# Partial sums by plain loads, earlier stream loads and spaced side work in a parallel retention and pooling layer

## The chip, the core and the metric

The kernel runs on one core of one Trainium2 chip. The metric is device time in microseconds (us) of the whole program. One execution was also taken by the hardware profiler, and all rows of the trace come from it.

## What is computed

The input is x, 2048 rows of 1024 numbers, in float32. With h the RMS norm of x, a projection gives six groups of 1024 columns: q, k, v, g_ret, u and g_pool.

```python
h = rms_norm(x, pre_g)
q, k, v, g_ret, u, g_pool = split(h @ w_in, 6)
y_ret = retention_branch(q, k, v, positions, ret_norm_g) * silu(g_ret)
y_pool = pooling_branch(u, pool_w, pool_scale) * silu(g_pool)
y = concatenate([y_ret, y_pool]) @ w_out
return x + rms_norm(y, post_g)
```

Retention has 8 heads of 128 columns: a rotary turn of q and k by the positions, products within chunks of 128 rows, a state carried from chunk to chunk, and a norm for each head. Pooling takes, for each quarter of u, a causal mean over 2, 4, 8 or 16 rows less the value itself, and multiplies it with a 256x256 matrix pool_w.

## The kernel before

**Units.** The sequence is cut into four blocks of 512 rows. The large products are done in units. A unit makes a 2x2 arrangement of 128x512 results with seven products in place of eight (a Strassen form), so it needs sums of its operands: S1, S2, S3 and S4. A product is 4 contraction tiles, and each is three matmuls of 128x512, since a float32 operand is split into an upper and a lower part (`split`, L142: ScalarE copies the upper part, VectorE subtracts it). So a unit is 7 x 4 x 3 = 84 matmuls of 512 columns.

**Phases.** There are four phases, and `line` lists their units in order. Phase 0 does blocks 0 and 1 (24 units: 16 for heads, 8 for pooling), phase 1 does blocks 2 and 3 (24 units). Phase 2 multiplies the first half of y with `w_out` for all rows (8 units) and stores partial sums in the DRAM tensor `part`. Phase 3 does the second half (8 units), adds `part`, and finishes the rows: the sum of squares, the norm, x added, the store to `out`. The first two units of phase 0 are done by `first()` (L829) in an order written out by hand (`manual_schedule`). All the rest is ordered by a planner: it takes the order of the program as priority, and puts an instruction into its engine's queue when by its own costs the operands and buffers are there. On the chip each queue is in order and waits where an operand is late.

**The loop** (L1080). For a unit it runs seven places, `at` = 0 to 6, with the products 6, 2, 5, 7, (1 of the next unit), 4, 3. After each product, `slot()` runs what was put off to this place by `later(i, f)` (i places on), then the chore listed for this place, and then `nxt.prep(at)`, the sums and splits of the next unit. At `at` = 6 it calls `load()` for the unit after the next: plain loads by the queue of SyncE (SP), and two accumulating DMAs by GpSimd (POOL), which add a second quadrant onto S1 and S3. `prep(0)` then adds S2 = S1 + "11" on VectorE.

**Buffers.** Operands of units (raw quadrants, sums, lower parts) live in 13 tiles `X`. Nearly everything else lives in 16 tiles `T`: rotated q and k, copies from PSUM, folds, results. A load waits in SP's queue until its tile is free.

**Chores of phase 0** prepare later phases, each in one go at its place in `chores` (L1067). `fold_pool_weights(g)` multiplies pool_w into the projection of u (four times; loads, splits with the lower part on POOL, 48 matmuls of 256 columns, copies by ScalarE, stores). `stats_next(b)` loads the rows of block 2 or 3 and squares them on ScalarE. `tables(b)` makes cosines and sines: eight VectorE steps, three on ScalarE. `combine_h(j)` scales transposed tiles of x for phase 1 and stores seven combinations into `made`; `combine_o` (in phase 1) does the like for `w_out`, for phases 2 and 3. When the phase changes, `after.fetch` loads and splits the seven resident operands of the new phase.

**Phase 3.** For the first seven units, `total(q)` copies or subtracts a result out of PSUM into a tile `ot`, and lets POOL accumulate `part` onto it by a DMA (L686). Two places later come the squares (L681) and `finish`: the norm (L715 to L726), x added by an accumulating DMA of POOL (L732), and right behind it the store `out` on SP's queue (L733). The last unit has a variant: `fetch` loads `part` plainly, `adjust` (L677, POOL) subtracts it from the two saved terms u2 and x5, and the other two results take it in a VectorE addition (`total_last`, L700).

**The saved terms.** Product 6's bank is corrected in place (L322) and copied to u2 by ScalarE (L324), then product 7 accumulates into the same bank. Product 5's bank is copied to x5 (L331), then product 3 accumulates into it.

Of the kernel before, what the change touches and what calls it, by code (L numbers as in the profile page):

```python
# [9 lines left out]
F32 = mybir.dt.float32  # L10
# [71 lines left out]
def layer_kernel(ctx: ExitStack, tc: tile.TileContext, x, xt, pos, wt, wut, wo, pw, cols, postg, const, out):  # L82
# [126 lines left out]
    def combine_tile(n, j, b11, b12, b21, b22, keep):  # L209

        s = slice((j % 2) * BLK, (j % 2 + 1) * BLK)

        def put(p, t):
            nc.gpsimd.dma_start(out=made[n, p][j // 2][:, s], in_=t)

        def op(p, a, b, alu):
            t = T(f"c{n}{p}{j}")[:, :BLK]
            nc.vector.tensor_tensor(out=t, in0=a, in1=b, op=alu)
            put(p, t)
            return t  # L220
        if keep:
            for p, t in ((1, b11), (2, b21), (3, b22)):
                put(p, t)
        t1 = op(5, b11, b12, ALU.subtract)
        t2 = op(6, b22, t1, ALU.add)
        op(7, b12, b22, ALU.subtract)
        op(4, b21, t2, ALU.subtract)

    def combine_h(j, b0, b1):
# [4 lines left out]
        for name, b, k in (("b11", b0, j), ("b12", b1, j), ("b22", b1, KH + j), ("b21", b0, KH + j)):  # L234
            nc.vector.scalar_tensor_tensor(out=t[name], in0=t[name], scalar=col[:, k:k + 1], in1=rb[b],
                                           op0=ALU.mult, op1=ALU.mult)
        combine_tile(1, j, t["b11"], t["b12"], t["b21"], t["b22"], True)

    def combine_o(n, j):
# [5 lines left out]
        combine_tile(n, j, t["b11"], t["b12"], t["b21"], t["b22"], False)  # L245


    class Unit:
        def __init__(self, name, quads, uses):
            self.name, self.quads, self.uses = name, quads, uses  # L250
            self.op, self.bank = {}, {}
            self.fetch = self.adjust = None

        def load(self):
            self.raw = {}

            def land(name, q):
                t, view = X(f"{name}_{self.name}"), self.quads[q]
                dst = t if len(view.shape) == 2 else t.rearrange("p (f t) -> p f t", f=KH)
                nc.sync.dma_start(out=dst, in_=view)  # L260
                self.raw[name] = t
                return dst
            s1 = land("S1", "21")
            s3 = land("S3", "11")
            nc.gpsimd.dma_start(out=s1, in_=self.quads["22"], accum_op=ALU.add)
            nc.gpsimd.dma_start(out=s3, in_=self.quads["21"], accum_op=ALU.add)
            for q in ("11", "12", "22"):
                land(q, q)
# [11 lines left out]
        def prep(self, i):  # L280
            raw = self.raw
            if i == 0:
# [856 lines left out]
```

## Time and profile before

| | us |
|---|---|
| median of 3 runs | 1624.98 (1624.18 to 1631.08) |
| time of the profiled execution | 1622.46 |
| its span, from first to last instruction | 1620.6 |
| TensorE (PE) busy in the span | 1473.8 |
| VectorE (DVE) busy | 1044.2 |
| ScalarE (ACT) busy | 722.6 |
| GpSimd (POOL) busy | 500.0 |

The mean granted clock of TensorE is 0.967 of 2.4 GHz. Two things are read from such a profile: where TensorE idles and what it waited for, stage by stage, and where its clock fell to the lower level behind such a wait.

### The profile page before, as it was taken

The page shows a single profiled execution, that of the slowest core. Times are in us where ns is not written, and L with a number is a line of the kernel's source. Part 1 is how long each engine was busy: PE and PEld are TensorE (multiplying, and loading weights), DVE is VectorE, ACT ScalarE, POOL GpSimd, SP SyncE. Part 2 cuts the span into 40 slices and gives each one's busy share as a digit, 9 for nine tenths or more (in the row PEclk, how much of TensorE's full clock was granted, in tenths as well). Part 3 has the DMA queues.
Part 4 walks back from the last instruction along what each step waited for, and adds up shares of the span by engine and source line. Part 5 has one row for each costly group of instructions (what it writes and reads, how often), then busy time and mean ns, then how long its engine had stood idle before and what let it go on. Part 6 is the DMA issues. An engine that isn't in the chain of part 4 may idle for free. (4 is left out here: it accounts for less than half of the span.)

```text
span 1620.6 us, 20953 instructions
## 1 busy us (share of the span) xinstructions
PE 1473.8 (91%) x6976; PEld 1209.9 (75%) x6976; DVE 1044.2 (64%) x2166; ACT 722.6 (45%) x1383; POOL 500.0 (31%) x529
## 2 busy tenths in 40 slices
PE   4998979898989999799999999999996999987875
PEld 3777767687878888588888887887885888766664
DVE  6983736775757766876777667677677544645354
ACT  5554535445344434454444444344444433533331
POOL 0223231325252425522223314233245221133333
PEclk9999999999999999799999999999998999998987
DMA  8134544546454546544455535554456655887976
GB/s 309 41 78 124 150 111 109 151 131 173 140 155 133 162 123 173 180 116 105 117 156 149 161 82 148 144 162 108 121 153 191 177 155 144 286 194 149 221 163 175
DMA packets 115372, 243.80 MB, mean 150 GB/s; under 512 B 14016, under 2 KB 14144, under 8 KB 115264
## 3 DMA queue, kind: packets, MB, share of 16 engines
q1 hardware_dynamic: 75264, 149.12, 28.3%
q0 software_dynamic: 40000, 93.35, 26.4%
q8 instruction: 55, 0.90, 0.2%
q14 instruction: 53, 0.43, 0.1%
HBM read 187.88 MB, written 54.53 MB: 150 GB/s over the span
## 5 line engine op out<-in xcount | busy, mean ns | idle before, releaser
L312 PE MATMUL b_o<-rh,h_o 128*128 128x512 f32 x192 | 82.9, 432 | 40.3 <-ACT u_o L324 24.6
L431 POOL TENSOR_TENSOR sw_q<-sw_q,sin 128x512 f32<-128x512 f32 x32 | 50.6, 1583 | 144.7 <-ACT sw_q L429 98.8
L312 PE MATMUL b_up<-rh,h_up 128*128 128x512 f32 x192 | 78.7, 410 | 18.0 <-DVE gp L336 13.4
L443 POOL DMA_DIRECT2D yd<-sg x32 | 25.0, 780 | 196.3 <-DVE r L487 145.1
L312 PE MATMUL b_qk<-rh,h_qk 128*128 128x512 f32 x180 | 74.3, 413 | 10.7 <-DVE rot_k L336 5.6
L313 PE MATMUL b_o<-rl,h_o 128*128 128x512 f32 x192 | 81.2, 423 | 0.5 <-DVE rl L145 0.5
L314 PE MATMUL b_o<-rh,l_o 128*128 128x512 f32 x192 | 80.7, 420 | 0.0
L517 ACT ACTIVATE on<-op,sh,y_o 128x128 f32<-128x128 f32 x128 | 48.1, 456 | 72.7 <-DVE sh L514 72.7
L312 PEld LDWEIGHTS b_o<-rh,h_o 128*128 128x128 f32 x192 | 39.4, 205 | 54.8 <-ACT u_o L324 27.5
L313 PE MATMUL b_up<-rl,h_up 128*128 128x512 f32 x192 | 77.5, 404 | 0.0
L314 PE MATMUL b_up<-rh,l_up 128*128 128x512 f32 x192 | 77.4, 403 | 0.0
L313 PE MATMUL b_qk<-rl,h_qk 128*128 128x512 f32 x180 | 72.6, 403 | 0.0
L312 PE MATMUL b_vg<-rh,h_vg 128*128 128x512 f32 x180 | 72.3, 402 | 0.2 <-DVE rot_q L430 0.2
L314 PE MATMUL b_qk<-rh,l_qk 128*128 128x512 f32 x180 | 72.3, 402 | 0.0
L314 PE MATMUL b_vg<-rh,l_vg 128*128 128x512 f32 x180 | 70.5, 392 | 0.0
L313 PE MATMUL b_vg<-rl,h_vg 128*128 128x512 f32 x180 | 70.3, 391 | 0.0
L624 POOL TENSOR_TENSOR w<-ub 128x527 f32<-128x527 f32 x32 | 41.3, 1290 | 86.8 <-issue 41.1
L624 POOL TENSOR_TENSOR w<-w 128x525 f32<-128x525 f32 (+2 forms) x48 | 66.5, 1386 | 2.4
L145 DVE TENSOR_TENSOR rl<-m,rh 128x1024 fp32r<-128x1024 f32 x42 | 57.3, 1369 | 15.3 <-ACT rh L144 13.5
L431 POOL TENSOR_TENSOR sw_k<-sw_k,sin 128x512 f32<-128x512 f32 x32 | 49.8, 1557 | 56.1 <-ACT sw_k L429 53.0
L312 PEld LDWEIGHTS b_up<-rh,h_up 128*128 128x128 f32 x192 | 37.7, 197 | 28.8 <-DVE gp L336 15.3
L661 POOL DMA_DIRECT2D part<-pt_o x32 | 17.6, 552 | 108.9 <-ACT pt_o L349 65.7
(507 smaller groups left out, 4820.1 us busy)
## 6 DMA issues: line engine op xcount, KB each, us to landing
m<-made SPq DMA_DIRECT2D x30, 512.0 KB, 6.0
made<-c POOLq DMA_DIRECT2D x48, 256.0 KB, 4.0
yd<-sg POOLq DMA_DIRECT2D x32, 256.0 KB, 2.8
S_up<-in_wt POOLq DMA_DIRECT2D x32, 256.0 KB, 5.6
yd<-mx POOLq DMA_DIRECT2D x32, 256.0 KB, 2.8
b<-in_wo SPq DMA_DIRECT2D x32, 256.0 KB, 4.0
S_o<-yd SPq DMA_DIRECT2D x32, 256.0 KB, 4.0
S_o<-yd POOLq DMA_DIRECT2D x32, 256.0 KB, 5.9
```

The source lines that it names most:

```text
L145: (eng or nc.vector).tensor_tensor(out=r32(lo), in0=val, in1=hi, op=ALU.subtract)
L312: nc.tensor.matmul(o, wh, mh, start=opens and j == 0, stop=False, **more)
L313: nc.tensor.matmul(o, wh, ml, start=False, stop=False, **more)
L314: nc.tensor.matmul(o, wl, mh, start=False, stop=j == KH - 1, **more)
L431: nc.gpsimd.tensor_tensor(out=sw, in0=sw, in1=tabs[b][1], op=ALU.mult)
L443: nc.gpsimd.dma_start(out=yd[b][:, :, f, :], in_=t.rearrange("p (c t) -> p c t", c=CPB))
L517: nc.scalar.activation(out=self.on[:, c], in_=op[:, c], func=AF.Identity, scale=rs[:, i:i + 1], bias=shift[:, i:i + 1])
L624: nc.gpsimd.tensor_tensor(out=dst[:, s0:], in0=src[:, s0:], in1=src[:, s0 - step:E - step], op=ALU.add)
L661: nc.gpsimd.dma_start(out=place(part, q), in_=t)
```

## The change

1. **Phase 3.** All eight units now take the way of the last one: `fetch` loads four tiles of `part` plainly, on SP's queue, at product 1. A new method `taken` makes u2 and x5 with one VectorE subtraction of `part` out of PSUM in place of ScalarE's copy and POOL's `adjust`. The other two results are VectorE additions. Squares follow at once. For the first seven units the store to `out` is put off four places.
2. **Loads.** S1 and S3 are loaded at `at` = 4, "11" and "22" at 5, "12" at 6. S2 is added in `prep(1)` and no longer in `prep(0)`.
3. **Chores in stages.** Folds, tables, statistics and combinations use `later` between load, split, product and store. Some start at other places: the four `combine_h` at units 8, 18, 19 and 20 (before: 10, 13, 16 and 19).
4. **Start.** In `first()`, the first row tile of x is loaded ahead of the constants. The lower parts of the weights (`rest_w`) are made on VectorE one step behind their upper parts on ScalarE.
5. **Positions** come from the host as 128 equal rows, so a load reads one row for each partition.

```diff
     class Unit:
...
-            self.fetch = self.adjust = None
+            self.fetch = self.part = None
...
+        def load_sums(self):
+            self.raw = {}
+            self.land("S1", "21", "22")
+            self.land("S3", "11", "21")
+        def load_rest(self, names):
+            for q in names:
+                self.land(q, q)
...
-            if i == 0:
-                self.add("S2", raw["S1"], raw["11"], nc.vector)
-            elif i == 1:
+            if i == 1:
+                h11 = raw["11"]
                 self.split(1, "11")
+                self.add("S2", raw["S1"], h11, nc.vector)
...
+        def taken(self, q, o, name):
+            t = T(f"{name}_{self.name}")[:, :BLK]
+            if self.part:
+                nc.vector.tensor_tensor(out=t, in0=o, in1=self.part[q], op=ALU.subtract)
+            else:
+                nc.scalar.copy(out=t, in_=o)
+            return t
...
         def total(q):
             def use(c, i):
-                o[q] = landed(c, i, f"ot{q}_{n}")
-                nc.gpsimd.dma_start(out=o[q], in_=place(part, q), accum_op=ALU.add)
...
+                t = o[q] = T(f"ot{q}_{n}")[:, :BLK]
+                if i:
+                    nc.vector.tensor_tensor(out=t, in0=c, in1=parts[q], op=ALU.add)
+                else:
+                    c(t)
...
+                nc.scalar.activation(out=parts[q], in_=t, func=AF.Square, scale=1.0 / 32.0,
+                                     accum_out=s2[:, k:k + 1])
...
                 elif q == "12":
-                    finish(("11", "12"))
+                    later(2, lambda: finish(("11", "22", "21", "12")))
...
-                nc.sync.dma_start(out=out[spot], in_=t)
+                if final:
+                    nc.sync.dma_start(out=out[spot], in_=t)
+                else:
+                    later(4, lambda t=t, spot=spot: nc.sync.dma_start(out=out[spot], in_=t))
...
     def fold_pool_weights(g):
-        pool = halves(f"p{g}", load_pool(g))
-        for dh in range(2):
-            fold_store(g, dh, fold_products(g, dh, pool, fold_split(g, dh, load_fold(g, dh))))
+        st = {"pr": load_pool(g), 0: load_fold(g, 0)}
...
+        later(2, begin)
+        later(3, lambda: operands(0))
+        later(6, lambda: multiply(0))
+        later(7, lambda: fold_store(g, 0, st[0]))
+        later(7, second)
+        later(10, lambda: operands(1))
+        later(13, lambda: multiply(1))
+        later(14, lambda: fold_store(g, 1, st[1]))
...
+        xs = {0: [row(0, 0)]}
         nc.sync.dma_start(out=cst, in_=const)
         load_pi(0)
-        xs = {0: rows(0)}
+        xs[0] += [row(0, st) for st in range(1, CPB)]
...
+            if i == 2:
+                rest_w(0, 1)
+                rest_w(1, 1)
+            elif i > 3 and i - 1 in upper:
+                rest_w(*upper[i - 1])
...
-                elif n + 2 < len(line):
-                    line[n + 2][2].load()
+                if n + 2 < len(line):
+                    ahead = line[n + 2][2]
+                    if at == 4:
+                        ahead.load_sums()
+                    elif at == 5:
+                        ahead.load_rest(("11", "22"))
+                    elif at == 6:
+                        ahead.load_rest(("12",))
```

In `stats_next` the loads come two to a place and each square three places behind its load; in `tables` the eight VectorE steps come two to a place, ScalarE's three at place 7 and the stores one later. In `combine_tile` two of the four results come at place 5 (3 for `combine_o`) and two one place later, each stored one place behind.

## Rows read from the trace of the kernel before

**Rows 1.** The page, busy time and share of the span by engine.

```profile
PE 1473.8 (91%) x6976; PEld 1209.9 (75%) x6976; DVE 1044.2 (64%) x2166; ACT 722.6 (45%) x1383; POOL 500.0 (31%) x529
```

**Rows 2.** Stretches: length; PE, PEld, DVE, ACT, POOL busy; PE clock; DMA; GB/s.

```profile
0.00:36.00 36.00, 14.87 (x46) 9.32 (x46) 22.31 (x54) 18.00 (x30) 0.20 (x4) 1.00 0.93 348
...
72.00:640.00 568.00, 527.36 (x2661) 437.57 (x2660) 373.06 (x854) 267.57 (x536) 185.94 (x195) 0.98 0.49 135
640.00:700.00 60.00, 48.44 (x180) 38.06 (x180) 50.12 (x55) 29.59 (x48) 33.21 (x27) 0.86 0.65 194
700.00:1200.00 500.00, 492.41 (x2488) 412.24 (x2487) 342.18 (x780) 227.12 (x438) 146.44 (x154) 1.00 0.48 128
...
1260.00:1400.00 140.00, 137.87 (x606) 113.20 (x605) 64.96 (x94) 56.98 (x94) 28.36 (x43) 1.00 0.63 182
...
1430.00:1607.00 177.00, 142.42 (x549) 112.17 (x547) 79.84 (x182) 58.43 (x129) 57.77 (x65) 0.89 0.80 178
```

**Rows 3.** Waits in phase 3, 1430 to 1607: who, for whom, us, times, longest.

```profile
DVE sS_o L272 <- DMA S_o<-yd: 41.7, 5, 10.3
...
PE b_o L312 <- ACT u_o L324: 20.4, 5, 6.1
```

**Rows 4.** Waits of SP's queue in phase 3, 1430 to 1607.

```profile
SPq L733 <- DMA ot_o<-in_x: 146.5, 22, 22.4
```

**Rows 5.** DMA in phase 3, 1430 to 1607: queues, then issues.

```profile
q0 software_dynamic: 9074, 16.52, 56.1%
q1 hardware_dynamic: 8173, 14.91, 23.2%
...
ot_o<-in_x POOLq DMA_DIRECT2D x28, 256.0 KB, 5.8
out<-ot_o SPq DMA_DIRECT2D x28, 256.0 KB, 5.2
ot_o<-part POOLq DMA_DIRECT2D x25, 256.0 KB, 6.5
...
S_o<-yd POOLq DMA_DIRECT2D x10, 256.0 KB, 5.7
```

**Rows 6.** PE's waits in phase 0, 72 to 640 us.

```profile
PE c_qk L312 <- ACT x_qk L331: 9.7, 4, 4.4
...
PE wf L773 <- ACT w110h L144: 4.2, 1, 4.2
PE wf L775 <- POOL w110l L145: 3.6, 1, 3.6
...
PE wf L773 <- ACT w101h L144: 0.3, 1, 0.3
```

**Rows 7.** ACT in order of time at two waits: start, duration, idle before.

```profile
309.71 0.72 ACT L407 ACTIVATE sd<-ang,cst 128x512 f32<-128x512 f32 x1 [2.46 <-DVE ang L821]
...
392.18 0.65 ACT L783 COPY wf<-wf 128x256 f32<-128x256 f32 x2 [2.76 <-PE wf L775]
```

**Rows 8.** Stretch 480 to 520, with one combine_h in it.

```profile
480.00:520.00 40.00, 39.44 (x208) 33.33 (x207) 28.34 (x64) 18.01 (x35) 10.00 (x13) 1.00 0.43 126
```

**Rows 9.** DVE in 480 to 520 by line: busy us, mean ns, idle before.

```profile
L235 DVE SCALAR_TENSOR_TENSOR b<-b,col,rb 128x512 f32<-128x512 f32 x4 | 2.8, 744 | 0.0
```

**Rows 10.** PE's waits in phase 1, 700 to 1200 us.

```profile
PE b_qk L312 <- DVE rot_k L336: 5.6, 3, 3.6
```

**Rows 11.** The start in order of time, engines mixed.

```profile
1.65 2.07 SPq L839 DMA_DIRECT2D xs<-in_x  x4
...
7.89 1.06 ACT L848 ACTIVATE xs<-xs 128x1024 f32<-128x1024 f32 x1 [5.66 <-DMA xs<-in_x]
...
29.53 0.50 PE L935 MATMUL f<-b21l,wh 128*128 128x512 f32 x1 [1.77 <-DVE b21l L922]
...
30.07 0.69 DVE L145 TENSOR_TENSOR wl<-w,wh 128x512 fp32r<-128x512 f32 x1 [0.60 <-ACT wh L144]
```

**Rows 12.** Waits of SP's queue over the whole span.

```profile
SPq L260 <- DVE l_qk L145: 157.5, 27, 14.7
```

More of the change, by code (lines that the diff above doesn't have):

```diff
@@ L216, in op @@
         def op(p, a, b, alu):
[L217 to L220, printed above, removed]
+            t = src[p] = T(f"c{n}{p}{j}")[:, :BLK]
+            nc.vector.tensor_tensor(out=t, in0=src[a], in1=src[b], op=alu)
+            later(1, lambda: put(p, t))
         if keep:
[L222 to L227, printed above, removed]
+            for p, name in ((1, "b11"), (2, "b21"), (3, "b22")):
+                later(5, lambda p=p, name=name: put(p, src[name]))
+        d = 5 if keep else 3
+        later(d, lambda: op(5, "b11", "b12", ALU.subtract))
+        later(d, lambda: op(6, "b22", 5, ALU.add))
+        later(d + 1, lambda: op(7, "b12", "b22", ALU.subtract))
+        later(d + 1, lambda: op(4, "b21", 6, ALU.subtract))
     def combine_h(j, b0, b1):
@@ L251, in __init__, with land @@
             self.op, self.bank = {}, {}
-            self.fetch = self.adjust = None
-        def load(self):
[L255 to L268, printed above, removed]
+            self.fetch = self.part = None
+        def land(self, name, q, more=None):
+            t, view = X(f"{name}_{self.name}"), self.quads[q]
+            dst = t if len(view.shape) == 2 else t.rearrange("p (f t) -> p f t", f=KH)
+            nc.sync.dma_start(out=dst, in_=view)
+            if more:
+                nc.gpsimd.dma_start(out=dst, in_=self.quads[more], accum_op=ALU.add)
+            self.raw[name] = t
+        def load_sums(self):
[5 more added lines that the diff above has]
+                self.land(q, q)
+        def load(self):
+            self.load_sums()
+            self.load_rest(("11", "22", "12"))
         def add(self, k, a, b, eng):
@@ L840, in load, with row @@
             return t
-        def rows(b):
-            return [load(wide(f"xs{b}{st}"), x[b * BLK + st * P:b * BLK + (st + 1) * P, :]) for st in range(CPB)]
+        def row(b, st):
+            return load(wide(f"xs{b}{st}"), x[b * BLK + st * P:b * BLK + (st + 1) * P, :])
         def square(b, st, t):
@@ L897, in first @@
                 load_w(k, q)
-        xs[1] = rows(1)
+        xs[1] = [row(1, st) for st in range(CPB)]
         load_pi(1)
```

156 lines of the change are left out of this document (78 added, 78 removed).

## The prediction

> **What bounds the kernel now.** The first view is the page's busy time: PE is busy in 91% of the span [rows 1]. So the other engines matter only where they make PE wait, and what the change can win lies in the 147 us in which PE stands still and in the slow matmuls behind such waits. The second view cuts the span into stretches [rows 2]. PE is idle for 21.1 us of the first 36 (36.00 less 14.87), 40.6 of the 568 us of phase 0, 11.6 of the 60 around the change to phase 1, 7.6 in the rest of phase 1, 2.1 in phase 2 and 34.6 in the last stretch, phase 3. The granted clock is 0.98 of 2.4 GHz over phase 0, 0.86 at the change of phase and 0.89 in phase 3; its low level is 1.2 GHz, so phase 0 loses 0.02 x 568 = 11.4 us more to matmuls at the low level. In phase 2 it stands at 1.00, and the units there are the same 84 matmuls as in phase 3. That gives a yardstick: phase 2 issues 606 matmuls in 140 us, 0.231 us each. At that pace the 549 of phase 3 take 126.8 us and not 177, so phase 3 loses 50 us. In units of 84 (549 / 84 = 6.54) it is 27.1 us for one where phase 2 needs 19.4.
>
> The third view is who waits for whom in phase 3. PE stands before product 7 for ScalarE's copy u2, that for VectorE's correction, and VectorE has stood in its queue for 41.7 us in all before S2, for the DMA that makes S1 [rows 3]. Why is S1 late? SP's own waits say it: in 177 us its queue stands 146.5 us before the stores to `out`, for the DMAs that add x [rows 4]. The loads of the next unit are queued behind. This is a wait, not work: the chain runs store, load, accumulate, S2, u2, PE.
>
> **Phase 3, part by part.** The change takes away four accumulations of `part` a unit and adds four plain loads, of equal size. Their price comes from the queues [rows 5]. POOL's queue was busy 0.561 x 177 = 99.3 us (all 16 engines together) with 28 + 25 + 10 = 63 accumulations: 1.58 us each. SP's queue was busy 0.232 x 177 = 41.1 us with 14.91 / 0.262 = 57 plain ones: 0.72 us each. So DMA took 140.4 / 6.54 = 21.5 us of a unit's 27.1. After the change a unit has 6 accumulations (two for sums, four for x) and 13 plain transfers (five loads, four of `part`, four stores): 6 x 1.58 + 13 x 0.72 = 18.9 us. That is just below PE's 19.4, so DMA stays nearly full and some waits must remain.
>
> The squares no longer wait for a DMA (6.5 us to land), so x is added earlier. The store moves four places, 4 x 19.4 / 7 = 11 us, which is more than the 5.8 us that adding x takes to land [rows 5]; behind it on SP's queue stand the next loads, and they also move up two places, 5.5 us. VectorE takes over four operations a unit from ScalarE. At 0.74 us each, the price of a like one [rows 9], that is 3.0 us for a unit; with its 79.8 us in this stretch it comes to 99 us of about 139, 71%, so it isn't the bound. The four loads of `part` stand on SP's queue ahead of the next sums, but are issued 4 places before their first use. Nothing in the change adds a wait to PE except that u2 now needs `part` and VectorE twice; the correction and the subtraction have two products, 5.5 us, before product 7.
>
> What a unit then takes lies between 19.4 (as in phase 2) and 27.1 less the DMA time saved, 27.1 - 2.6 = 24.5 (the chain stays and only gets shorter). I take a quarter of the way from 19.4 to 27.1, since a DMA share of 0.63 cost phase 2 next to nothing and the share here would be 18.9 / 21.3 = 0.89: 21.3 us. Gain 177 - 6.54 x 21.3 = 38 us, with ends of 50 and 17.
>
> A rule speaks against this part. The row shows an accumulation at 1.58 us and a plain transfer at 0.72, on the same 16 engines [rows 5]. The Trainium skill, in DMA: Bandwidth & Descriptors, "Issuing engines are not separate DMA queues", says that DMAs from any issuing engine run on the same 16 DMA engines and that issuing from several saves only issue time. Taken alone it would leave DMA at 21.5 us a unit (a rival below); the trace agrees that the engines are shared, but not that the transfers cost the same.
>
> **Phase 0.** PE's waits [rows 6] name two chores. Fifteen rows of fold matmuls, from 4.2 us down to 0.3, sum to 16.2 us: the products stand in PE's queue before the splits are made. Product 3 waits 9.7 us for the copy x5, and ACT's order says why: its copy stood behind fold copies that waited 2.76 us for PE, and another time behind the sine of `tables`, which waited 2.46 us for VectorE's angle [rows 7]. With three places (8 us) between split and product, and one between product and copy, both go. That is 25.9 of 40.6 us idle; the like part (64%) of the clock's 11.4 us is 7.3. Together 33 us.
>
> Against it stand two costs. The last three `combine_h` now lie one unit apart. Each is four scalings at 0.74 us [rows 9] and four combinations, taken alike: 5.9 us of VectorE. With one of them VectorE had 28.3 us of 40 and PE lost 0.6 [rows 8]; with two it would have 34.2, 86%. The nearest row for that is the change of phase, 50.1 of 60 us, 84%, where PE loses 11.6 us and the clock 0.14 x 60 = 8.4. So it costs between 0 and 20 us; I take 5, because POOL, busy 33.2 of 60 there [rows 2], is busy 10.0 of 40 here. The second cost is tiles: stages hold the 16 tiles `T` longer, and each fold holds some five for 14 places. No row shows such a wait; I take 8 us, about two waits of the length of the longest in rows 6, with ends of 0 and 20. Gain 33 - 5 - 8 = 20 us, ends 35 gained and 5 lost.
>
> **Loads, positions, the other stages.** Moving loads up two places should do nothing in phases 0 to 2. SP waits there for a free tile `X` (157.5 us for one kind of split alone [rows 12]), so a load already goes out as soon as a tile is free. I count 0, and S2 one place later has the whole product before product 6 as cover; if that cover is gone, it costs the wait itself, as in rows 3. The positions read the same bytes: 0. The staged `combine_o` should remove most of phase 1's 5.6 us [rows 10], in which VectorE was late: 4 us, ends 0 and 7.6. The changes of phase keep their bursts of splits: 0.
>
> **Start.** The first row tile of x leaves SP's queue ahead of two loads; it left at 1.65 us and the first square began at 7.89 [rows 11]. At most 1.65 us come of it, but four squares follow each other and the last row tile lands no earlier: 1 us. In the first products VectorE waits 0.60 us for ScalarE at each of four weight splits, and PE waits for VectorE, 1.77 us the longest time [rows 11]; one step later the upper part is there: 4 x 0.60 = 2.4, of which 2 us. Together 3 us, ends 0 and 5.
>
> **Sum.** 38 + 20 + 4 + 3 = 65 us. The profiled execution took 1622.46 us, 1.9 more than its span, so 1557.5 after; the median of the runs is 2.5 above the profiled one, so 1560.
>
> **Rivals.**
> SP still blocked: the planner puts an instruction where its own clock calls it ready, so a store put off in the program may stand in SP's queue where it stood. For it: loads ran ahead to the first free tile [rows 12]. Against: nothing delays adding x any more by squares that wait for a DMA. Then a unit takes 24.5 us, phase 3 gains 17, and the time is 1581.
>
> A transfer costs what it did, and the queue it goes by is all that changes: DMA stays at 21.5 us a unit, at a share of 0.89 a unit is 24.2 us, phase 3 gains 19, the time is 1579. Rows 5 speak against it. [...]
>
> Phase 0 gives nothing: the stages end the fold waits and new ones take their place. For it: VectorE at 86% and tiles held longer. Time 1580.
>
> Slower: tiles `T` run out. In phase 3 an output tile is held 11 us longer and four tiles of `part` come four places early; at `at` = 6 I count 15 of 16 in use (four outputs not yet stored, four new, four `part` for the next unit and one for the last square, u2, x1). If a unit needs one more than there is, PE's feeders wait for a store to land. One such wait is priced at 4.2 us, the longest of rows 6, and 11.4 / 40.6 of that for the clock: 5.4 us. The 65 us are eaten at 12 waits; one in every second of the 30 units of phases 0 and 3 costs 81 us, and the time is 1641. Against it: SP's wait before the stores [rows 4] is for data, not for a tile. The Trainium skill, in Perfetto Trace Analysis, "Optimization Strategy", says that the same gap repeated on the engine that should be saturated can mean too few buffers for the next tile; by that, phase 3's repeated gaps would come from tiles and the change would make them worse.
>
> **How the numbers follow.** Chances: the forecast 0.55, SP still blocked 0.15, equal transfer cost 0.07, phase 0 gives nothing 0.13, tiles run out 0.10. The best ends give 50 + 35 + 7.6 + 5 = 98 us, 1527; the high end, 1602, takes in the three rivals near 1580 and most of their bounds, and leaves out the tiles. Half a per cent, 8 us, is about what a measurement can tell from no change: faster than 1617 has 0.87, within 0.04, slower 0.09.
>
> **What would show it.** Right: SP's wait before L733 falls from 146.5 us to under 30, VectorE's before S2 from 41.7 to under 15, the fold rows of PE's waits to under 5 in sum, no wait of product 3 for x5 over 1 us, phase 3 at 21 us a unit with DMA near 0.9, the clock near 1.00 in phase 0, the first product a microsecond earlier. Wrong: units of phase 3 at 24 us or more, waits for the release of a tile `T` ahead of PE's feeders, or a stretch with VectorE over 85% around units 18 to 20 in which PE idles.

## The result and the profile after

The changed kernel takes 1525.15 us (median of 4 runs, 1522.23 to 1529.36) against 1628.03 beside it; the ratio is 0.937, 95% interval 0.933 to 0.941. Its profiled execution took 1523.67 us with a span of 1521.9. Between the two profiled executions 98.8 us are gone, where 65 were predicted. The page of the changed kernel, busy time by engine:

```profile
PE 1440.0 (95%) x6976; PEld 1194.4 (78%) x6976; DVE 1065.5 (70%) x2196; ACT 708.4 (47%) x1353; POOL 473.4 (31%) x499
```

The matmuls are as many as before, 6976, and yet PE is busy for 33.8 us less than in [rows 1]: they ran less often at the lower clock (the mean granted clock rose from 0.967 to 0.985 of 2.4 GHz). Stretches of the changed kernel, columns as in [rows 2]; the lines are the start, phase 0, the change to phase 1, a part of phase 1, phase 2 and phase 3:

```profile
0.00:36.00 36.00, 17.93 (x62) 13.43 (x63) 25.34 (x62) 21.83 (x38) 0.20 (x4) 1.00 0.91 346
69.00:620.50 551.50, 532.39 (x2728) 446.12 (x2727) 404.63 (x874) 277.17 (x556) 203.04 (x209) 0.99 0.53 148
620.50:700.00 79.50, 76.79 (x379) 62.55 (x378) 59.52 (x118) 44.39 (x76) 27.70 (x22) 1.00 0.50 139
700.00:1200.00 500.00, 487.08 (x2413) 407.06 (x2412) 355.86 (x744) 230.04 (x439) 164.37 (x172) 0.99 0.52 143
1219.10:1333.60 114.50, 114.50 (x505) 94.53 (x505) 53.83 (x77) 47.28 (x78) 23.69 (x36) 1.00 0.62 178
1333.60:1506.30 172.70, 159.67 (x673) 129.51 (x671) 114.08 (x237) 63.65 (x129) 36.77 (x43) 0.96 0.85 227
```

To compare stages I count the products' 512-column matmuls, 84 to a unit, and take the times at which units start. The 22 units of phase 0 that the planner orders go from 72.2 to 669.8 us before and from 69.0 to 620.5 after. "Change" is the last unit of phase 1 and two of phase 2. "Phase 3" is the last unit of phase 2, at 19.3 us wherever the new loads are and about 22 elsewhere, and phase 3's eight. "Tail" is what follows the start of the last matmul. Five units of phase 2 took 95.2 us in every kernel. Stages are of the one execution that was profiled, medians of all. The kernel before was profiled in an execution of 1622.46 us, 4 to 6 below its medians beside the experiments, so gains by stages often sum to less than gains by medians. All numbers are us:

| kernel | start | phase 0 | phase 1 | change | phase 3 | tail | median | ratio, 95% |
|---|---|---|---|---|---|---|---|---|
| before | 72.2 | 597.7 | 537.0 | 76.2 | 227.9 | 14.5 | 1628.03 | 1 |
| after | 69.0 | 551.5 | 528.5 | 70.1 | 191.3 | 16.2 | 1525.15 | .933-.941 |
| e1 chores only | 72.0 | 563.6 | 534.8 | 76.2 | 233.1 | 14.9 | 1590.41 | .977-.980 |
| e2 phase 3 only | 72.1 | 596.3 | 536.9 | 76.2 | 215.2 | 16.5 | 1612.87 | .989-.994 |
| e3 loads only | 72.3 | 592.8 | 536.4 | 71.2 | 231.1 | 14.4 | 1611.05 | .989-.992 |
| e4 start only | 68.8 | 595.1 | 539.4 | 77.0 | 228.6 | 14.4 | 1620.46 | .994-.998 |
| e5 phase 3 and loads | 72.2 | 595.5 | 537.1 | 72.8 | 191.3 | 15.5 | 1575.96 | .964-.971 |
| e6 store at once | 68.9 | 548.7 | 529.2 | 71.0 | 208.7 | 16.0 | 1540.77 | .944-.948 |
| e7 constants first | 68.4 | 548.3 | 529.1 | 69.5 | 188.3 | 16.2 | 1521.85 | .932-.938 |
| e8 accumulate kept | 68.6 | 548.4 | 529.5 | 70.4 | 217.0 | 15.2 | 1546.1 | .947-.952 |
| e9 fold steps together | 68.8 | 578.1 | 527.3 | 70.5 | 192.5 | 16.0 | 1550.45 | .951-.956 |
| e10 stats, tables in one | 68.5 | 556.4 | 528.7 | 69.7 | 190.3 | 16.0 | 1532.65 | .939-.946 |
| e11 15 tiles | 68.8 | 555.7 | 531.1 | 70.1 | 189.4 | 16.0 | 1525.74 | .936-.941 |
| e12 combine in one | 68.3 | 554.8 | 538.6 | 69.2 | 191.2 | 16.0 | 1534.07 | .939-.946 |
| e13 loads undone | 68.9 | 558.5 | 534.8 | 76.4 | 215.4 | 15.9 | 1568.43 | .960-.969 |
| b1 finish later | 68.2 | 551.8 | 528.7 | 70.3 | 190.5 | 16.2 | 1523.29 | .931-.939 |
| b2 finish in two | 68.4 | 549.1 | 530.3 | 70.4 | 190.2 | 16.0 | 1523.36 | .932-.940 |
| b3 store later | 68.1 | 551.3 | 528.5 | 72.6 | 195.5 | 16.0 | 1526.62 | .935-.940 |
| b4 loads together | 67.6 | 548.4 | 528.9 | 70.0 | 194.3 | 16.0 | 1525.37 | .935-.940 |

After, e6 to e8 and b1 to b3 share phase 0's code, and it took them 548.3 to 551.8 us: a stage of one profile says nothing below about 4 us. In phase 3 the old code of before, e1 and e4 took 227.9 to 233.1, so there it is about 5.

By this table the change gained 3.2 us at the start, 46.2 in phase 0, 8.5 in phase 1, 6.1 in the change, 36.6 in phase 3, and lost 1.7 in the tail.

**Phase 0 in five parts.** The same units of both kernels (four, four, eight, five, and the last one); columns as above. Before:

```profile
72.20:195.10 122.90, 112.38 (x593) 93.01 (x590) 81.94 (x195) 66.32 (x130) 33.19 (x32) 0.97 0.44 115
195.10:319.20 124.10, 107.18 (x525) 87.38 (x524) 76.85 (x202) 57.08 (x119) 32.62 (x35) 0.95 0.47 126
319.20:529.10 209.90, 198.28 (x1023) 166.38 (x1022) 134.25 (x305) 92.97 (x184) 76.97 (x82) 0.99 0.51 146
529.10:637.20 108.10, 106.52 (x512) 88.26 (x511) 77.14 (x150) 49.35 (x101) 41.73 (x43) 1.00 0.50 140
637.20:669.80 32.60, 24.70 (x86) 19.34 (x85) 24.48 (x26) 13.18 (x23) 20.11 (x17) 0.79 0.65 186
```

After:

```profile
69.00:180.00 111.00, 106.34 (x578) 89.00 (x576) 81.97 (x189) 60.51 (x111) 31.99 (x30) 1.00 0.43 109
180.00:277.30 97.30, 95.52 (x489) 79.83 (x488) 69.35 (x194) 53.94 (x120) 23.69 (x26) 1.00 0.51 149
277.30:476.70 199.40, 197.16 (x1048) 167.59 (x1046) 141.24 (x305) 98.62 (x197) 74.69 (x75) 1.00 0.50 133
476.70:590.60 113.90, 109.47 (x535) 91.03 (x534) 90.20 (x164) 51.56 (x107) 52.68 (x63) 1.00 0.66 195
590.60:620.50 29.90, 23.89 (x86) 18.67 (x86) 21.87 (x25) 12.54 (x23) 19.99 (x18) 0.83 0.70 208
```

Length less PE's busy time is PE's idle time: 10.5, 16.9, 11.6, 1.6 and 7.9 us before, 4.7, 1.8, 2.2, 4.4 and 6.0 after. In sum 48.5 became 19.1. The clock stood at 0.95 to 0.99 of 2.4 GHz in the first three parts and now stands at 1.00. In six slices of 20 to 24 us of the second part it had stood at 0.83 where PE idled 9.3 us, at 0.87 where it idled 4.4, and at 1.00 in the other four: a mean of time at 2.4 and at 1.2 GHz. Two of the six:

```profile
215.00:235.00 20.00, 10.71 (x66) 9.38 (x65) 2.64 (x5) 6.30 (x15) 8.54 (x10) 0.83 0.49 121
...
255.00:275.00 20.00, 20.00 (x102) 16.45 (x102) 12.65 (x45) 10.91 (x28) 1.82 (x2) 1.00 0.44 106
```

So 29.4 us of the gain are idle time and 16.7 are PE's busy time, 549.06 to 532.39 us. (An estimate from the rounded clocks of the parts, their shortfall times their length, gives 18.8 us lost before and 5.1 after, about 14 of the 16.7.) The fourth part, in which three `combine_h` now lie one unit apart, is the one place that got worse: by 5.8 us, of which 3.0 are PE's busy time (fold matmuls that moved there: x512 to x535) and 2.8 idle time.

**Phase 3.** Waits of the changed kernel in its window, 1333.6 to 1506.3, in the form of [rows 3, 4] (of PE, VectorE and SP):

```profile
PE b_o L330 <- DVE ot_o L348: 11.1, 3, 4.4
...
DVE sS_o L281 <- DMA S_o<-yd: 8.1, 4, 2.9
```

```profile
SPq L726 <- DMA ot_o<-in_x: 70.4, 22, 14.0
```

Before, from 1430 to 1607, PE had a second long wait beside those of rows 3. It is for the result "22", which VectorE must read before product 4 accumulates into the same bank (L336 before, L348 after):

```profile
PE b_o L312 <- DVE ot_o L336: 14.0, 6, 4.9
```

PE's wait for u2 (20.4 us in rows 3) is gone, that for "22" fell only from 14.0 us to 11.1, VectorE's wait for S1 fell from 41.7 us to 8.1, and SP's wait before the stores from 146.5 to 70.4. The DMA queues there, in the form of [rows 5]:

```profile
q1 hardware_dynamic: 14421, 27.36, 44.9%
q0 software_dynamic: 6264, 11.70, 40.2%
```

### The profile page after: what moved, and what is told of

Read it like the earlier page. It is cut to its first block, busy times and chain, and to the rows that moved or that the text cites. A ratio compares the mean times of both kernels' runs of the same rounds, so it can differ in the third digit from the quotient of the medians.

```text
span 1521.9 us, 20927 instructions
## 1 busy us (share of the span) xinstructions
PE 1440.0 (95%) x6976; PEld 1194.4 (78%) x6976; DVE 1065.5 (70%) x2196; ACT 708.4 (47%) x1353; POOL 473.4 (31%) x499
## 5 line engine op out<-in xcount | busy, mean ns | idle before, releaser
L330 PE MATMUL b_o<-rh,h_o 128*128 128x512 f32 x192 | 78.0, 406 | 14.1 <-DVE ot_o L348 11.1
L524 ACT ACTIVATE on<-op,sh,y_o 128x128 f32<-128x128 f32 x128 | 48.2, 457 | 68.6 <-DVE sh L521 68.6
L331 PE MATMUL b_o<-rl,h_o 128*128 128x512 f32 x192 | 76.8, 400 | 0.0
L332 PE MATMUL b_o<-rh,l_o 128*128 128x512 f32 x192 | 76.5, 399 | 0.0
L330 PE MATMUL b_qk<-rh,h_qk 128*128 128x512 f32 x180 | 72.1, 401 | 3.8 <-ACT u_qk L315 2.5
L332 PE MATMUL b_vg<-rh,l_vg 128*128 128x512 f32 x180 | 70.5, 392 | 0.0
L332 PE MATMUL b_qk<-rh,l_qk 128*128 128x512 f32 x180 | 70.5, 391 | 0.0
L145 DVE TENSOR_TENSOR rl<-m,rh 128x1024 fp32r<-128x1024 f32 x42 | 52.2, 1244 | 17.9 <-ACT rh L144 15.0
L330 PE MATMUL a_o<-rh,h_o 128*128 128x512 f32 x128 | 50.0, 390 | 1.9 <-ACT x_o L338 1.9
```

The source lines that it names most:

```text
L145: (eng or nc.vector).tensor_tensor(out=r32(lo), in0=val, in1=hi, op=ALU.subtract)
L330: nc.tensor.matmul(o, wh, mh, start=opens and j == 0, stop=False, **more)
L331: nc.tensor.matmul(o, wh, ml, start=False, stop=False, **more)
L332: nc.tensor.matmul(o, wl, mh, start=False, stop=j == KH - 1, **more)
L524: nc.scalar.activation(out=self.on[:, c], in_=op[:, c], func=AF.Identity, scale=rs[:, i:i + 1], bias=shift[:, i:i + 1])
```

## The experiments

**Which part brings what.** Four kernels are the kernel before with one part of the change each: the staged chores with the new positions, phase 3, the loads, the start with the new positions. Their core lines, in this order:

```diff
+        later(3, lambda: operands(0))
+        later(6, lambda: multiply(0))
```

> The kernel before with the staged chores alone (folds, tables, statistics, combinations, with their new places; positions by partition). Theory A: nearly all of what phase 0 gave (46 us) and phase 1 (10 us) comes of the chores, so about 50 us faster, 1578. Theory B: the part of phase 0's gain that the forecast did not have (46 against 20) comes of the earlier loads and the later S2, so about 20 to 25 us faster, 1604.

```diff
+            u.fetch, u.part = fetch, parts
+                    later(4, lambda t=t, spot=spot: nc.sync.dma_start(out=out[spot], in_=t))
```

> The kernel before with the change of phase 3 alone (partial sums by plain loads, squares at once, stores four places later), loads of S1 and S3 where they were. Theory A: the store in front of the loads and the accumulations were the cause, so nearly all of phase 3's 34 us, at least 28 us faster. Theory B: the loads two places up are needed for it as well, since SP's queue still holds the stores in front of them: 10 to 20 us faster.

```diff
+                    if at == 4:
+                        ahead.load_sums()
```

> The kernel before with the loads two products up and S2 one place later, alone. Theory A: loads are bound by free operand tiles and not by their place, so phases 0 to 2 give within 3 us of nothing, and phase 3 gives a few us since the loads stand ahead of the stores: 0 to 10 us faster. Theory B: phase 0 gains 20 us or more by it, 20 to 35 us faster.

```diff
+        xs = {0: [row(0, 0)]}
+                rest_w(*upper[i - 1])
```

> The kernel before with the change of the start alone (first row tile ahead of the constants, lower parts of the weights one step later, positions by partition). Both theories: 3 to 4 us faster, all of it before 72 us, with the first square 3 us earlier and the first product 0.7 us later, as in the trace after.

They gain 36.6, 14.1, 15.9 and 6.5 us (medians against 1626.96), 73 together, where the change gains 103. So e2 came out as its theory B has it, e1 and e3 lie between their two theories, and e4 gained more than the 3 to 4 us of both. By stages the chores gain 34.1 us in phase 0, phase 3's part only 12.7 in phase 3, the loads 4.9 in phase 0 and 5.0 at the change, the start 3.4. (For e3 all stages together give 7.2 us, so where the rest of its 15.9 lies isn't known.) What single parts leave out is an interplay, and most of it lies in phase 3, where the four add up to 3.6 of the 36.6 us. Some 8 us more are in phase 1, where they add up to 0.5 of the 8.5.

```diff
+            u.fetch, u.part = fetch, parts
+                        ahead.load_sums()
```

> The kernel before with the change of phase 3 and the earlier loads together, chores and start as before. Alone they gave 12.7 us (phase 3) and -3.2 us (loads) in phase 3's stretch. Theory A, the two need each other: phase 3's stretch gives the 36.5 us of the changed kernel, the whole 48 to 55 us faster. Theory B, the rest of phase 3's gain needs the chores or the start (another order of the planner): 15 us in phase 3, about 28 us faster.

Phase 3's part and the loads together give phase 3 all it has in the changed kernel, 191.3 us: 36.6 gained where 12.7 and a loss of 3.2 stood alone (the loss is within what phase 3 of the old code varies). Theory A holds. The chores and the start add nothing there.

**What carries phase 3.** In the changed kernel one step is undone at a time: the store's delay, then the plain loads of `part` (POOL accumulates `part` as before, squares two places later; u2 and x5 are ScalarE's copies again).

```diff
-                if final:
-                    nc.sync.dma_start(out=out[spot], in_=t)
-                else:
-                    later(4, lambda t=t, spot=spot: nc.sync.dma_start(out=out[spot], in_=t))
+                nc.sync.dma_start(out=out[spot], in_=t)
```

> The changed kernel with the store to out right behind the DMA that adds x, not four places later. Theory A, the loads two places up are what brings them ahead of the stores, and the planner places a store when it is ready whatever its place in the program: within 5 us of the changed kernel, 1525 to 1530. Theory B, the four places are what frees the queue: phase 3 loses 15 us or more, 1540 or more.

```diff
+                o[q] = landed(c, i, f"ot{q}_{n}")
+                nc.gpsimd.dma_start(out=o[q], in_=place(part, q), accum_op=ALU.add)
+                later(2, sq)
+        if not final:
+            return Unit(n, quads, {q: total_acc(q) for q in quads})
```

> The changed kernel, but the first seven units of phase 3 add the partial sums by accumulating DMAs as before, with squares two places later; the stores stay four places later and the loads two products up. Theory A, the order on SP's queue was the main cause: phase 3 keeps half of its gain or more (DMA floor 22 us a unit at 6.5 units, so 15 to 20 us slower than the changed kernel, 1540 to 1545). Theory B, the price and the waits of the accumulations were the main cause: phase 3 falls back nearly to the kernel before, 30 us slower or more, 1555.

The first gives back 17.4 us of phase 3, as its theory B has it. Its waits, 1332.3 to 1521.9:

```profile
SPq L723 <- DMA ot_o<-in_x: 112.0, 28, 15.8
```

```profile
DVE l_o L145 <- ACT h_o L144: 20.5, 7, 5.6
```

SP stands 112.0 us before the stores (70.4 in the changed kernel). ScalarE stands 23.5 us for "11", a load behind them (4.1), VectorE 20.5 for ScalarE's upper parts (7.5), and PE 18.0 for "22" (11.1).

The second gives back 25.7 us, and its median, 1546.1, lies between its two theories, nearer to A. Issues of POOL and then waits, 1331.3 to 1529.3:

```profile
ot_o<-part POOLq DMA_DIRECT2D x28, 256.0 KB, 9.7
...
S_o<-yd POOLq DMA_DIRECT2D x13, 256.0 KB, 12.4
```

```profile
ACT sq_o L736 <- DMA ot_o<-part: 55.8, 22, 7.3
...
DVE l_o L145 <- ACT h_o L144: 46.8, 12, 6.1
...
PE b_o L330 <- DVE ot_o L348: 27.5, 6, 5.9
```

The sums' accumulation lands 12.4 us after its issue, against 8.3 in the changed kernel and 5.7 in rows 5. Yet VectorE has no wait for S1 there. What it waits for are ScalarE's upper parts (46.8 us) and "12" (19.0). ScalarE in turn stands 55.8 us before its squares, until `part` has landed on the result, and the copies of upper parts are queued behind. So the squares that wait for a DMA in ScalarE's queue are a second link of the kind that SP's stores are. By the prices below, 28 accumulations are also 45 us of all 16 engines and 28 plain loads 21; how much of the 25.7 us is that price and how much the squares, no run separates.

**Loads undone in the complete change.**

```diff
-                    if at == 4:
-                        ahead.load_sums()
-                    elif at == 5:
-                        ahead.load_rest(("11", "22"))
+                elif n + 2 < len(line):
+                    line[n + 2][2].load()
```

> The changed kernel with the old loads: all five at the last place, S2 added one product earlier. Theory A, phase 3's gain hangs on the loads and so do some of the other stages': phase 3 gains about 13 us and not 36, the change between phases 1 and 2 loses its 6, phase 0 about 5, so some 1558 us. Rival B, the loads matter in phase 3 alone: 1549. Rival C, with the chores spaced the loads add nothing anywhere but the change of phase: 1531.

43.3 us slower than the changed kernel: 24.1 in phase 3, 7.0 in phase 0, 6.3 in phase 1, 6.3 at the change. Theory A, with more of it than expected. (S2 also stands one product earlier again, so the run undoes both.) VectorE's waits for loads between 69 and 1175 us show where the sums came late, first with the old loads, then in the changed kernel:

```profile
DVE sS_vg L276 <- DMA S_vg<-in_wt: 5.5, 3, 2.4
DVE sS_up L276 <- DMA S_up<-in_wt: 5.4, 5, 1.8
...
DVE sS_qk L276 <- DMA S_qk<-in_wt: 1.6, 1, 1.6
```

```profile
DVE sS_vg L281 <- DMA S_vg<-in_wt: 0.7, 1, 0.7
```

S1 is two transfers in series, the load and the accumulation on it; S2 waited 12.5 us for them with the old loads, and 0.7 in the changed kernel. With the loads as the only change (e3) it is 0.6, though phases 0 and 1 gain only 4.9 and 0.6 us there.

**What carries phase 0.** In the changed kernel the fold's split, products and copies go to one place again, while their start places stay; then statistics and tables go in one piece; then the combinations (the first `combine_h` at the place where its scalings were).

```diff
-        later(6, lambda: multiply(0))
-        later(7, lambda: fold_store(g, 0, st[0]))
+        later(3, lambda: multiply(0))
+        later(3, lambda: fold_store(g, 0, st[0]))
```

> The changed kernel, but in each half of a fold the split, the products and the copies stand at one place (3 and 10), where the changed kernel has 3, 6, 7 and 10, 13, 14; loads stay early. Theory A, the distance between split and product is what took 26 us of waits (fold matmuls for splits, product 3 for the copy x5 behind the fold copies) out of phase 0: fold rows of PE's waits come back to 8 us or more and phase 0 gets 15 to 30 us longer. Theory B, early loads are enough and the steps may stand together: within 5 us.

```diff
-        for i in range(4):
-            later(2 + i, lambda i=i: turn(steps[2 * i:2 * i + 2]))
-        later(7, trig)
+        for step in angles(pi, ang, kk):
+            step()
```

> The changed kernel with the statistics (eight loads and eight squares at one place) and the tables (eight VectorE and three ScalarE steps at one place) in one go as before, at the new places. Theory A, these bursts are the part of phase 0's gain that the forecast did not count (about 13 to 20 us): phase 0 that much longer. Theory B, bursts on ScalarE and VectorE of 6 us are hidden by the products: within 5 us, and the uncounted part is only the 13 us of costs that were taken off the forecast and did not come.

```diff
-        later(3, lambda: scaled((("b11", b0, j), ("b12", b1, j))))
-        later(4, lambda: scaled((("b22", b1, KH + j), ("b21", b0, KH + j))))
-        combine_tile(1, j, t, True)
+            nc.vector.scalar_tensor_tensor(out=t[name], in0=t[name], scalar=col[:, k:k + 1], in1=rb[b],
+                                           op0=ALU.mult, op1=ALU.mult)
+        combine_tile(1, j, t["b11"], t["b12"], t["b21"], t["b22"], True)
```

> The changed kernel with each combine_h and combine_o in one go (four loads, four scalings, four combinations and the stores at one place, as before), at the new units. Theory A, a burst of 6 us on VectorE delays rotated k and the corrections, as the waits of phase 1 show: 5 to 15 us slower, most of it around units 18 to 21 of phase 0 and in phase 1's units with combine_o. Theory B, VectorE has room for it: within 3 us.

The folds' distances alone are worth 26.6 us of phase 0, theory A. The longest of PE's waits for folds with the fold steps together, 69 to 647 us, then the longest in the changed kernel, 69 to 620.5:

```profile
PE wf L764 <- ACT w200h L144: 2.6, 1, 2.6
PE wf L764 <- ACT w210h L144: 2.2, 1, 2.2
PE wf L764 <- ACT w310h L144: 2.0, 1, 2.0
```

```profile
PE wf L766 <- POOL w001l L145: 1.4, 1, 1.4
```

That is the wait of rows 6 again: the fold rows sum to 19.1 us here, to 16.2 before and to 2.3 in the changed kernel. PE's wait for x5 does not come back with them. With statistics and tables in one piece it comes back in part, 3.7 us of the 9.7 of rows 6:

```profile
PE c_qk L330 <- ACT x_qk L315: 3.7, 1, 3.7
```

Statistics and tables are worth 4.9 us in phase 0, the combinations 3.3 there, both near what a stage of one profile can tell, and the combinations 10.1 in phase 1. By the medians the two cost 7.5 and 8.9 us: between its theories for the first, theory A for the second, though in phase 1 and not in phase 0. One thing stays untested. Folds, statistics and tables also start at other units (three of the four folds one to four units later, the tables four), and no run puts these places back.

**Tiles.**

```diff
-NX, NXH, NT = 13, 6, 16
+NX, NXH, NT = 13, 6, 15
```

> The changed kernel with 15 tiles T in place of 16. Theory A, tiles are not what anything waits for (the 8 us taken off the forecast for them were wrong): within 5 us of 1525. Theory B, the stages and the partial sums use all 16 and one less makes PE's feeders wait: 10 us slower or more, in phase 0 and phase 3.

With one tile `T` less the time is the same, 1525.74 us, theory A. The planner found an order that does without the sixteenth, so the tiles `T` don't run out, in phase 0 or in phase 3.

**The start.** Constants and positions again ahead of all four row tiles:

```diff
-        xs = {0: [row(0, 0)]}
-        xs[0] += [row(0, st) for st in range(1, CPB)]
+        xs = {0: [row(0, st) for st in range(CPB)]}
```

> The changed kernel with the constants and the positions loaded ahead of all four row tiles, as before; the lower parts of the weights still one step later. Theory A, the later row tiles behind the constants set the first product, and moving one tile ahead only delays them: first product at 15.8 us and not 16.6, the whole 0.7 us faster. Theory B, the first square sets it: 2 us or more slower.

The first row tiles in the changed kernel, then with that step undone:

```profile
4.53 1.06 ACT L855 ACTIVATE xs<-xs 128x1024 f32<-128x1024 f32 x1 [2.29 <-DMA xs<-in_x]
...
9.90 1.06 ACT L855 ACTIVATE xs<-xs 128x1024 f32<-128x1024 f32 x1 [4.22 <-DMA xs<-in_x]
...
12.46 1.06 ACT L855 ACTIVATE xs<-xs 128x1024 f32<-128x1024 f32 x1
```

```profile
8.03 1.06 ACT L855 ACTIVATE xs<-xs 128x1024 f32<-128x1024 f32 x1 [5.79 <-DMA xs<-in_x]
...
11.86 1.06 ACT L855 ACTIVATE xs<-xs 128x1024 f32<-128x1024 f32 x1
```

The first square came 3.4 us earlier (4.53; 7.89 in rows 11), but the second waited until 9.90, and the last began at 12.46 against 11.86. So the row tile put first made the first product later, 16.57 us against 15.96, and the start's gain is all from the lower parts of the weights (the new positions with the old start, e1, gave 0.2 us). In total time the step makes no difference that shows.

**What is left of phase 3.** It still takes 172 us for eight units where phase 2's pace gives 152. In the 172.7 us of its window PE idles 13.0; the other 7, by estimate, are the clock, 0.96 there. One of the three remaining stalls of PE for "22" begins at 1390.47 and lasts 4.42 us. VectorE of the changed kernel before it, in order of time:

```profile
1384.70 0.69 DVE L281 TENSOR_TENSOR sS_o<-S_o,11_o 128x512 f32<-128x512 f32 x1 [2.93 <-DMA S_o<-yd]
...
1388.67 0.69 DVE L281 TENSOR_TENSOR sS_o<-sS_o,12_o 128x512 f32<-128x512 f32 x1 [2.61 <-DMA 12_o<-yd]
...
1391.51 2.73 DVE L716 SCALAR_TENSOR_TENSOR ot_o<-ot_o,y_fo,pg 128x512 f32<-128x512 f32 x4
1394.16 0.68 DVE L348 TENSOR_TENSOR ot_o<-b_o,x_o 128x512 f32<-128x512 f32 x1
```

VectorE stands for S1, then for "12", then does four scalings (`finish`), and only then "22", which must be read before product 4 goes on in its bank. Four kernels, all with e7's start, move one of these each: `finish` to three places (with the stores at the place that they had), half of `finish` one place on, the store to six places, "12" loaded with "11" and "22".

```diff
-                    later(2, lambda: finish(("11", "22", "21", "12")))
+                    later(3, lambda: finish(("11", "22", "21", "12")))
```

> The changed kernel with the constants and positions again ahead of the four row tiles, and in phase 3 finish (the scalings and x) put off three places in place of two, the stores three in place of four. Theory A, the stalls left in phase 3 come from VectorE's queue, where S2's wait for its DMA and then the four scalings stand ahead of the correction of product 6's bank: with the scalings one place later they stand behind it, PE's wait on VectorE's result tiles falls from 11.1 us to under 4, and phase 3 from 188 us to about 180, the total to about 1512. Rival B, DMA at a share of 0.85 sets the pace: x is added one place later, the wait moves to S2 or to the next load, and phase 3 stays at 188 us (1521) or is longer.

```diff
+                if final or q in ("11", "22"):
+                    scaled()
+                else:
+                    later(1, scaled)
```

> As the former, but two of the four scalings stay where they were and two come one place later, each with its x and its store behind it. Theory A: the burst ahead of the correction is half as long (1.4 us and not 2.7), PE's wait for result tiles falls from 11.1 us to about 6 and phase 3 from 188 us to about 184, the total to about 1517. Rival B: phase 3 stays at 188 us, the total at 1521.

```diff
-                    later(4, lambda t=t, spot=spot: nc.sync.dma_start(out=out[spot], in_=t))
+                    later(6, lambda t=t, spot=spot: nc.sync.dma_start(out=out[spot], in_=t))
```

> The changed kernel with the constants and positions ahead of the four row tiles, and in phase 3 the stores to out put off six places in place of four. Theory A, what is left of phase 3's loss is still SP's queue: it stands 70.4 us before these stores in the changed kernel, the 12 load of the next unit behind it, and S2 and the next sum wait for that (2.93 and 2.61 us at one place); two places later x has landed, SP's wait falls under 30 us, phase 3 from 188 to about 180 us, the total to 1513. Rival B, the DMA engines' load (share 0.85) makes the sums late whatever the order: SP's wait falls, phase 3 stays at 188 us, 1521.

```diff
-                        ahead.load_rest(("11", "22"))
-                    elif at == 6:
-                        ahead.load_rest(("12",))
+                        ahead.load_rest(("11", "12", "22"))
```

> As the former but with the stores four places off, and 12 loaded at place 5 together with 11 and 22 (place 6 before). Theory A: the 12 load gets ahead of the stores in SP's queue, the wait of the second sum goes (2.6 us at one place), phase 3 falls to about 184 us, the total to 1517. Rival B: tiles X are free no earlier, SP's queue stands for them and everything else behind, phase 3 stays at 188 us or is longer, 1521 or more.

All four are within 5 us of e7 (1521.85) and of the changed kernel; theory A fails each time. With `finish` later the same place in VectorE's order looks like this:

```profile
1386.38 0.69 DVE L281 TENSOR_TENSOR sS_o<-S_o,11_o 128x512 f32<-128x512 f32 x1 [3.93 <-DMA S_o<-yd]
...
1389.98 0.69 DVE L281 TENSOR_TENSOR sS_o<-sS_o,12_o 128x512 f32<-128x512 f32 x1 [2.83 <-DMA 12_o<-yd]
...
1394.47 2.74 DVE L716 SCALAR_TENSOR_TENSOR ot_o<-ot_o,y_fo,pg 128x512 f32<-128x512 f32 x4
1397.13 0.68 DVE L348 TENSOR_TENSOR ot_o<-b_o,x_o 128x512 f32<-128x512 f32 x1
```

The scalings still stand ahead of that result, presumably since the planner orders by its own clock, in which S1 isn't late; and the waits for DMA ahead of them grew. So b1 did not test the scalings' place, only that a distance in the program need not become one in the queue. In b3 and b4 SP's waits before the stores came out longer, 92.2 and 97.9 us, not shorter, and the sums' accumulations landed sooner, 5.1 us after issue and not 8.3, yet phase 3 was no shorter. Whether the rest of phase 3's loss is the DMA engines' load (share 0.85) or the order, these runs don't settle: rival B's times came out, but no run changed the load alone. No version beats the changed kernel by more than the runs differ.

## Why the prediction was right and wrong

The direction held, and the time was missed: 1560 predicted, 1525.15 measured, just below the range's low end of 1527. The profiled executions differ by 33.8 us more than the sum's 65: phase 0 gave 26.2 more than it was given, the change to phase 2 gave 6.1, phase 1 4.5, and phase 3 with the tail 3.1 less. By the steps:

- **Phase 3, 38 us: right.** 34.9 with the tail. A unit takes 172 / 8 = 21.5 us where 21.3 was said. That it is so near is partly luck: the quarter of the way from 19.4 to 27.1 was a choice with no row behind it. The prices held too: POOL's queue was busy 0.402 x 172.7 = 69.4 us with 28 + 13 accumulations and two stores of `part`, 1.61 us each by issues and 1.55 by bytes (11.70 / 0.262 = 44.7 transfers; 1.58 before), SP's 0.449 x 172.7 = 77.5 us with 27.36 / 0.262 = 104 transfers, 0.75 each (0.72). DMA took 0.851 x 172.7 / 8 = 18.4 us a unit, where 18.9 was said. That refutes the rival of equal transfer costs. The chain too was named rightly: e2 and e6 each leave one of its links and lose 24 and 17 us. What it lacked is ScalarE's queue, where squares stood for `part` (e8), and PE's wait for "22", which is most of what is left. Not right was one sign: SP's wait before L726 fell to 70.4 us and not under 30, though VectorE's wait for S1 fell under 15 (8.1). The blocked queue remained and mattered less once the loads were early: with the old ones (e2) SP waits 112.1 us there and VectorE still 27.3 for S1.
- **Phase 0, 20 us: the step that failed; it gave 46.2.** The mechanism was right for the folds: their waits fell from 16.2 us to 2.3 (under 5 was said), and with the steps together they come back (e9). No wait for x5 is left either, but the reason given for it holds in part only: the fold steps don't bring it back, the tables bring back 3.7 us of 9.7, and the rest stays open. Three terms were mis-sized. The idle time removed was taken as 25.9 us, from the two waits named; it was 29.4, with what the new packing cost already in it. The clock was taken as 64% of 11.4 us, 7.3; PE's busy time fell by 16.7. I had assumed that dips behind the waits I didn't name stay; the first three parts went to 1.00 altogether. (The last unit, beyond the window's end at 640, gave 2.7 us of the 46.2.) And of the 13 us that were taken off for costs, the 8 for tiles did not come and the 5 for packing came by about half. The chores alone bring 34.1 of the 46.2 us (e1), so even without the loads the stage lay near the best end that was given for it, 35.
- **Tiles, 8 us against: wrong.** They cost nothing (e11). I had counted occupancy without a row that shows a wait for a tile, and priced a wait that I had no sign of.
- **Packing of `combine_h`, 5 us against: about half came.** Idle time in the units around it rose from 1.6 to 4.4 us; the rest of the stretch's 5.8 us is fold matmuls that moved there. VectorE reached 53.40 of 67.00 us, 80%, where 86% was worked out.
- **Loads, 0 in phases 0 to 2: wrong.** e13 shows 19.6 us there (7.0, 6.3 and 6.3) beside the 24.1 in phase 3. The argument was that SP waits for a free tile and so a load already goes out as early as it can [rows 12]. The wait was there, but it did not show that the loads came early enough: the sums that hang on them were late (12.5 us of VectorE's waits in e13, 0.7 after).
- **Phase 1, 4 us: direction right, size low.** 8.5 were measured. Undoing the staged combinations costs 10.1 there (e12) and undoing the loads 6.3 (e13), but alone the chores gain 2.2 (e1) and the loads 0.6 (e3): they need each other, as in phase 3. Why they do stays open.
- **Start, 3 us: right for half the reason.** 3.2 were measured, all of it from the weights; the row tile cost 0.6 us where the sum had a gain of 1, and the first product came at 16.57 us, not earlier than the 15.84 of before.
- **Phase changes, 0: wrong for the one to phase 2,** 6.1 us, by the loads (e3 alone 5.0, e13 without them none). PE's longest wait there, for a result `gp` that VectorE takes out of PSUM, fell from 8.1 us to 2.8; how the loads bring that was not followed further. The tail lost 1.7 us, which no step had.
- **The rivals.** "SP still blocked" is true of the queue and false of the time. "Tiles" and "phase 0 gives nothing" are refuted by e11 and by the table. By the Trainium skill's rule on repeated gaps (Perfetto Trace Analysis, "Optimization Strategy") phase 3's gaps could have come from too few buffers; for the tiles `T` of the changed kernel the runs do not agree, since 15 give 1525.74 us and 16 give 1525.15. The tiles `X` and the banks were not varied.

The range failed for the same reason as the sum: its low end took 35 us as the best that phase 0 could give, the named waits alone without costs, and no end at all for the loads.

## What to carry to other kernels

Where short stalls leave an engine at its lower clock, take as the best case the whole of the stage's idle time and the whole of its clock loss, not the rows that you can name. A cost that no row shows belongs in the range and not in the sum. And a queue in order serves one stuck instruction at a time, a store that waits in SP's queue as well as a square that waits in ScalarE's: what a change gains there shows only when the loads behind it move and the store ahead of it moves too, so size such parts together.

## What the hardware showed beyond that

- One load put ahead of two others brought its data 3.4 us earlier, and the three that followed it later: the fourth square began at 12.46 us against 11.86.
- An accumulation takes longer to land behind others that POOL has just issued. In the changed kernel six accumulations of the sums went out right behind four for x (1374 to 1420), and four went out with none of these in flight (1444 to 1474). The views of the tile `S_o` on POOL in these two windows end with:

```profile
DMA to landing us min/median/max: 9.2/10.8/12.1
```

```profile
DMA to landing us min/median/max: 4.6/5.8/6.6
```

  The DMA share alone does not do it: b3 and b4 have 0.83 in phase 3 and a median of 5.1 us, the changed kernel 0.85 and 8.3. The price of each on the engines stayed at 1.5 to 1.6 us.
- Between two distances of a store, four places and six, SP's wait before it rose from 70.4 to 92.2 us (68.9 in e7, which has four places and the start of the second), and b4 has 97.9 at four places: in a queue that a planner orders, the wait need not follow the distance that the program gives.
